# The first load of a batched matmul: 2 KB packets in place of 8 KB ones

## The chip, the cores and the metric

One core of a Trainium2 chip. The time is the device time of one execution in microseconds. A ratio of two kernels is the mean time of one kernel's fast runs over that of the other's of the same rounds, so it isn't quite the ratio of the medians that are quoted beside it.

## The reference

```python
batch, m, k, n = 16, 512, 512, 512
a: (batch, k, m) float32;  b: (batch, k, n) float32
out = np.matmul(a.transpose(0, 2, 1), b).astype(np.float32)
```

It reads 2 x 16.8 MB and writes 16.8 MB.

## The kernel before

SyncE issues all loads and stores. VectorE casts them to bf16, TensorE multiplies, ScalarE copies PSUM to SBUF. The batches go in pairs. The first pair is loaded batch by batch, in four loads of 1 MB (`a` of batch 0, `b` of batch 0, `a` and `b` of batch 1), so that the compute can begin early. In these loads partition p holds the rows 4p to 4p + 3 of k, a contiguous run of 8 KB:

```python
R, RV = 8, 4
in0_v = [x.rearrange("batch (p r) m -> batch p r m", r=RV) for x in (a, b)]
...
for j in range(2):        # j = 0: a, j = 1: b, of batch 0
    nc.sync.dma_start(x_ts[j][:, 0:RV, :], in0_v[j][0]).then_inc(s_f[j], 16)
for j in range(2):        # of batch 1
    nc.sync.dma_start(x_ts[j][:, RV:R, :], in0_v[j][1]).then_inc(s_x[j], 16)
for n in range(2, 2 * pairs):
    if n >= NX:           # from the third pair on: wait until a buffer has been cast
        nc.sync.wait_ge(s_in, n - NX + 1)
    ...                   # 2 MB loads of 16 KB runs
```

All outputs are issued after the last load.

## Time and profile before

| | before |
|---|---|
| time, median of the first 3 runs | 123.19 us (123.08 to 123.24) |
| span of the profiled run | 121.4 us |
| DMA packets, bytes | 4864, 50.33 MB |
| share of the 16 DMA engines | 97.7% |
| busiest compute engine | PE, 51% |

Each digit of the DMA row on the page is the busy share of one of 40 equal slices, in tenths; the row of GB/s below it is what they moved. The DMA row is 9 from end to end here. The reading, which the experiments below bear out for this kernel, is that a microsecond more of transfer is a microsecond more of time (where the last output landed 4.07 us later, the time grew by 3.84), and all else is hidden behind it. The lines themselves are shown in the prediction.

### The profile page before, as it was taken

Reading aid. Unit: us, or ns where it says so; the run is one execution under the profiler, and the core shown is the slowest. Engines: PE = TensorE matmul, PEld = TensorE weight load, DVE = VectorE, ACT = ScalarE, POOL = GpSimd, SP = SyncE. Lnnn points to the kernel's source line nnn. Section 1 sums busy time; section 2 is a strip of 40 time slices with the busy share of each in tenths; the row PEclk is TensorE's granted clock in tenths of the full one; section 3 lists DMA queues with packets and bytes.
Section 4 is the critical chain, followed back from the end, with each engine's and each line's share of the span. In section 5 each row is a group of like instructions: output and inputs, shape, how many; then the busy total and the mean of one; then the engine's idle time right before and its main releaser. Section 6 shows DMA issues by size and latency. Waiting matters only on the chain.

```text
span 121.4 us, 1204 instructions
## 1 busy us (share of the span) xinstructions
PE 61.7 (51%) x480; PEld 35.0 (29%) x480; DVE 38.1 (31%) x48; ACT 32.2 (27%) x41; POOL 0.2 (0%) x4
## 2 busy tenths in 40 slices
PE   0007829099379559959919979989800000000000
PEld 0002314066156225536515636655400000000000
DVE  0061160864284090484265347492000000000000
ACT  4000423302900920390560084190009200000000
POOL 0000000000000000000000000000000000000000
PEclk9999999999999967999995999999995555555555
DMA  2999999999999999999999999999999999999994
GB/s 57 424 432 429 467 432 432 432 432 432 432 432 432 432 432 427 432 432 416 432 427 427 432 432 402 432 427 427 429 429 432 429 429 432 421 424 429 429 424 208
DMA packets 4864, 50.33 MB, mean 415 GB/s; under 512 B 384, under 2 KB 384, under 8 KB 384
## 3 DMA queue, kind: packets, MB, share of 16 engines
q1 hardware_dynamic: 4864, 50.33, 97.7%
HBM read 33.55 MB, written 16.78 MB: 415 GB/s over the span
## 4 chain that ended last, share of the span: by engine, by line
DMA 63%; DVE 6%; issue 3%; ACT 2%; SPq 2%; ACTq 1%
DMA x<-in_b_dram 53%; DMA out_dram<-o 10%; DVE bbf L118 3%; DVE abf L118 3%; ACT o L181 2%; SPq L74 1%; ACTq L70 1%; SPq L72 1%; SPq L80 0%; DVE done L124 0%; ACT done L186 0%; SPq L219 0%; SPq L70 0%
## 5 line engine op out<-in xcount | busy, mean ns | idle before, releaser
L156 PE MATMUL ps<-bbf,abf 64*128 64x512 bf16 x448 | 53.0, 393 | 13.6 <-PEq L151 13.6
L156 PEld LDWEIGHTS ps<-bbf,abf 64*128 64x128 bf16 x448 | 31.3, 112 | 35.3 <-issue 20.6
L181 ACT COPY o<-ps 128x1024 f32<-128x1024 f32 x28 | 26.3, 1026 | 45.9 <-PE ps L156 37.0
L118 DVE CAST abf<-x 128x2048 bf16<-128x2048 f32 x14 | 17.1, 1224 | 17.5 <-PE ps L156 13.5
L118 DVE CAST bbf<-x 128x2048 bf16<-128x2048 f32 x14 | 17.1, 1225 | 14.6 <-DMA x<-in_b_dram 14.6
L136 PE MATMUL ps<-bbf,abf 128*128 128x512 bf16 x32 | 8.7, 433 | 12.4 <-PEq L134 12.4
L136 PEld LDWEIGHTS ps<-bbf,abf 128*128 128x128 bf16 x32 | 3.7, 121 | 16.9 <-issue 14.8
L175 ACT COPY o<-ps 128x1024 f32<-128x1024 f32 x4 | 4.0, 1012 | 15.9 <-PE ps L136 15.9
L99 DVE CAST abf<-x 128x2048 bf16<-128x2048 f32 x2 | 2.5, 1228 | 11.2 <-DMA x<-in_a_dram 5.8
L99 DVE CAST bbf<-x 128x2048 bf16<-128x2048 f32 x2 | 2.5, 1225 | 1.2 <-DMA x<-in_b_dram 1.2
L186 ACT ACTIVATE done<-done 1x1 uint32<-1x1 uint32 x8 | 1.6, 197 | 0.0
L175 ACT ACT_TABLE_LOAD x1 | 1.3, 1283 | 0.9 <-SPq L70 0.9
L124 DVE MEMSET done<- 1x1 f32 x14 | 0.8, 59 | 0.0
L103 DVE MEMSET done<- 1x1 f32 x2 | 0.1, 59 | 0.0
L208 POOL MEMSET const-bfloat16-1.0<- 128x1 bf16 x1 | 0.1, 102 | 0.0
L208 POOL MEMSET const-uint8-127<- 128x1 uint8 x1 | 0.1, 102 | 0.0
L208 POOL MEMSET const-float32-0.0<- 128x1 f32 x1 | 0.1, 99 | 0.2 <-issue 0.2
L208 POOL MEMSET const-float32-1.0<- 128x1 f32 x1 | 0.1, 99 | 0.0
## 6 DMA issues: line engine op xcount, KB each, us to landing
x<-in_a_dram SPq DMA_DIRECT2D x7, 2048.0 KB, 12.2
x<-in_b_dram SPq DMA_DIRECT2D x6, 2048.0 KB, 15.9
out_dram<-o SPq DMA_DIRECT2D x3, 4096.0 KB, 21.7
x<-in_b_dram SPq DMA_DIRECT2D x4, 1024.0 KB, 12.1
out_dram<-o SPq DMA_DIRECT2D x2, 2048.0 KB, 29.3
x<-in_a_dram SPq DMA_DIRECT2D x2, 1024.0 KB, 6.8
```

Of the source, the lines that this page charges most:

```text
L70: with tc.tile_critical(no_gpsimd_drain=True):
L72: nc.sync.dma_start(x_ts[j][:, 0:RV, :], in0_v[j][0]).then_inc(s_f[j], 16)
L74: nc.sync.dma_start(x_ts[j][:, RV:R, :], in0_v[j][1]).then_inc(s_x[j], 16)
L99: nc.vector.tensor_copy(out=bf_ts[0][:], in_=x_ts[j][:, u * RV:(u + 1) * RV, :]).then_inc(s_cast, 1)
L118: nc.vector.tensor_copy(out=(bbf_ts if n % 2 else abf_ts)[v][:], in_=x_ts[n % NX][:, v * RV:(v + 1) * RV, :],).then_inc(s_cast, 1)
L124: nc.vector.memset(dve_done[:, n:n + 1], 0.0).then_inc(s_in, 1)
L136: mm = nc.tensor.matmul(ps_ts[0][h][:, t % 2, :], a_m[:, r, t], bbf_ts[0][:, r, :], start=(r == 0), stop=(r == RV - 1),)
L156: mm = nc.tensor.matmul(ps_ts[g][h][:, t % 2, :], a_m[:, t], bbf_ts[v][rows, r, :], start=(v == 0 and r == 0), stop=(v == V - 1 and r == R ...
L175: nc.scalar.copy(out=o_ts[0][:, g, 2 * h:2 * h + 2, :], in_=ps_ts[0][h][:]).then_inc(s_ev[h], 1)
L181: ev = nc.scalar.copy(out=o_ts[i % NO][:, g, 2 * h:2 * h + 2, :], in_=ps_ts[g][h][:])
L186: nc.scalar.memzero(act_done[:, i:i + 1]).then_inc(s_out, 1)
L208: nc = _bacc.Bacc("TRN2", target_bir_lowering=False, num_devices=1)
```

## The change

The intent is a gentler start: the very first load of the kernel runs on idle DMA engines (0 GB/s up to 1.9 us), and smaller packets could complete sooner there. The cap of 4 * M = 2048 bytes on a contiguous run cuts this one load into a packet per row: 512 packets of 2 KB where there had been 128 of 8 KB. Bytes, addresses and order of the loads stay as they were.

```diff
         for j in range(2):
-            nc.sync.dma_start(x_ts[j][:, 0:RV, :], in0_v[j][0]).then_inc(s_f[j], 16)
+            nc.sync.dma_start(
+                x_ts[j][:, 0:RV, :], in0_v[j][0], max_dma_last_dim=None if j else 4 * M
+            ).then_inc(s_f[j], 16)
```

## The prediction

> **What bounds the kernel now.** I read the busy table first, then the 40 slices, to see whether one resource is full from end to end.
>
> ```profile
> PE 61.7 (51%) x480; PEld 35.0 (29%) x480; DVE 38.1 (31%) x48; ACT 32.2 (27%) x41; POOL 0.2 (0%) x4
> ...
> DMA  2999999999999999999999999999999999999994
> GB/s 57 424 432 429 467 432 432 432 432 432 432 432 432 432 432 427 432 432 416 432 427 427 432 432 402 432 427 427 429 429 432 429 429 432 421 424 429 429 424 208
> DMA packets 4864, 50.33 MB, mean 415 GB/s; under 512 B 384, under 2 KB 384, under 8 KB 384
> ## 3 DMA queue, kind: packets, MB, share of 16 engines
> q1 hardware_dynamic: 4864, 50.33, 97.7%
> ```
>
> No compute engine is busy for much more than half of the span. The 16 DMA engines are busy in every slice but the first and the last, at about 430 GB/s, and 97.7% over the whole span. 50.33 MB at 430 GB/s is 117.0 us of the 121.4 us span. The other 4.4 us are the start before data flows at full rate and the tail after the last packet. So the end is set by two things only: when each DMA engine gets going, and how long its fixed list of packets takes. The chain of waits agrees: 63% of it is transfers, and its earliest stretch is the issue of the first six loads, one after the other.
>
> Then the start, in the timeline and in a table of short windows (columns of the latter: window, length, busy time of PE, PEld, DVE, ACT, POOL, clock, DMA share, GB/s).
>
> ```profile
> 0.94 0.39 SPq L72 DMA_DIRECT2D x<-in_a_dram  x1
> 1.39 0.42 SPq L72 DMA_DIRECT2D x<-in_b_dram  x1
> 1.86 0.42 SPq L74 DMA_DIRECT2D x<-in_a_dram  x1
> 2.33 0.66 SPq L74 DMA_DIRECT2D x<-in_b_dram  x1
> ...
> 5.78 1.23 DVE L99 CAST abf<-x 128x2048 bf16<-128x2048 f32 x1 [5.78 <-DMA x<-in_a_dram]
> 8.19 1.23 DVE L99 CAST bbf<-x 128x2048 bf16<-128x2048 f32 x1 [1.18 <-DMA x<-in_b_dram]
> ...
> 9.71 5.07 PE L136 MATMUL ps<-bbf,abf 128*128 128x512 bf16 x16 [9.71 <-PEq L134]
> ...
> 16.10 0.33 SPq L80 DMA_DIRECT2D x<-in_a_dram  x1
> ```
>
> ```profile
> 1.50:1.90 0.40, 0.00 (x0) 0.00 (x0) 0.00 (x0) 0.40 (x1) 0.00 (x0) 1.00 0.00 0
> 1.90:2.20 0.30, 0.00 (x0) 0.00 (x0) 0.00 (x0) 0.28 (x1) 0.00 (x0) 1.00 1.09 164
> 2.20:2.50 0.30, 0.00 (x0) 0.00 (x0) 0.00 (x0) 0.00 (x0) 0.00 (x0) 1.00 0.65 109
> 2.50:2.80 0.30, 0.00 (x0) 0.00 (x0) 0.00 (x0) 0.00 (x0) 0.00 (x0) 1.00 0.73 218
> 2.80:3.10 0.30, 0.00 (x0) 0.00 (x0) 0.00 (x0) 0.00 (x0) 0.00 (x0) 1.00 0.35 137
> 3.10:3.40 0.30, 0.00 (x0) 0.00 (x0) 0.00 (x0) 0.00 (x0) 0.00 (x0) 1.00 1.03 437
> ```
>
> The first load is issued at 0.94 us. Nothing moves until 1.9, and from 1.9 to 3.1 the engines move only (164 + 109 + 218 + 137) x 0.3 = 188 KB where 430 GB/s would have moved 516 KB. From 3.1 on the rate is full. So the ramp loses 0.76 us. The packet records of the trace show what that ramp is made of: the first packets start between 1.97 and 2.72 us, and several take 0.8 to 1.16 us each, where the 8 KB packet takes 309 ns in steady running.
>
> [...] an 8 KB packet takes 309 ns and a 16 KB packet 611, so 2 x 309 - 611 = 7 ns is the fixed part. [...] the 1 MB loads land in issue order, about 2.4 us apart (5.78, then 8.19). [...] In the trace each of these loads counts 16 completions. So both kernels give every engine the same 64 KB of the first a; only the cut into packets changes. [...]
>
> **The change, part by part.** In the kernel before, partition p holds rows 4p to 4p + 3 of the first a, one run of 8 KB. The change caps a run at 4M = 2048 bytes, one row. It moves the same bytes to the same places: no instruction of any compute engine changes, and no other DMA. The first a becomes 512 packets in place of 128. The page should show 4864 + 384 = 5248 packets.
>
> (a) Fixed cost per packet. With 7 ns fixed and (309 - 7) / 4 = 75.5 ns for the bytes, an estimated 82.5 ns a packet. Each engine now has 32 x 82.5 = 2.64 us instead of 8 x 309 = 2.47: **+0.17 us**. All 16 engines work side by side, so it counts once. It lies on the path, because the engines have no idle time later in which to make it up.
>
> (b) [...] The out transfers of this kernel have 512 packets too. Their issue instructions take 403, 507 and 870 ns for the first three, which are all out of the way 1.87 us after the first began; the loads with 128 packets take 327 to 433 ns late in the kernel. So 1536 descriptors were taken in 1.87 us, 1.2 ns each at most, and 384 more cost at most 0.47 us. [...] I take **+0.2 us**, between 0 and 0.47.
>
> (c) A gentler ramp. Smaller first packets complete sooner, and an engine with a slow first packet might lose less. The most that this can give is the 0.76 us of the ramp. But the slow packets all end close to 3.0 to 3.1 us, whether they began at 1.98 or at 2.65, as though they waited for one common event, and a smaller packet would wait for it too. I take **-0.15 us**.
>
> Sum: 0.17 + 0.2 - 0.15 = +0.22 us, so 123.19 + 0.22 = **123.4 us**.
>
> What lies off the path: when the first a lands. Even if it lands 0.4 us later, its cast (1.23 us from 5.78) ends at about 7.4, before the first b arrives at 8.19, and the first matmul waits for the latter's cast. [...] The cast chain then issues the next load at 16.10, while what was issued in the first 4 us (8.4 MB) keeps the DMA engines fed until 22.8: 6.7 us of slack, far more than any shift here.
>
> **The rivals.** Rival 1: the 2 KB packets start much faster, most of the ramp goes and the transfer time stays: -0.6 us, 122.6. For it speak first packets of up to 1.16 us; against it, their common end. Rival 2: [...] If the spread of 0.75 us in first starts (1.97 to 2.72) grew fourfold, the last engine would start 2.2 us late and never catch up: 125.5. Against it speak the issue times of the out transfers in (b). [...] Rival 4: the change is absorbed, because the early loads run far ahead of the compute: 123.2. The full DMA slices speak against it: with no idle slot between start and end there is nothing to absorb into, though it would look nearly the same in the time.
>
> **Range and chances.** The parts give -0.4 at the good end ((a) paid, (b) nil, two thirds of the ramp saved) and +0.8 at the bad end ((a) doubled, (b) at its limit), so 122.8 to 124.2 with a little room. 2% of 123.19 is 2.46 us. A gain of that size isn't there: the whole ramp is 0.76 us, and the time from the issue to the first packet is not touched. [...] So faster 0.005, same 0.975, slower 0.02.
>
> **What would show it right or wrong.** Right: 5248 packets; the first a landing within half a microsecond of 5.78; the landing of the first b, and every later landing, shifted by nearly the same amount as the end; steady slices unchanged near 430 GB/s; 2 KB packets of some 80 to 85 ns once running. Wrong: (a) falls if these packets take well over 85 ns in steady running; (b) if the first packets of the last engines start over half a microsecond later; (c) if the windows from 1.9 to 3.1 us carry far more than 188 KB. The claim that the shift passes to the end undiminished falls if the first b lands later but the last out lands as before. The prediction as a whole would be wrong if a feed gap opened near 22 us, or if the second load's issue were held up by the first for microseconds.

The sum came to 0.17 + 0.2 - 0.15 = +0.22 us, 123.4 us. (a) is an estimate from the durations of 309 and 611 ns, and the counts per engine (64 KB; 8 or 32 packets) are estimates too, an even split of each load over its 16 completions. For (b), +0.2 is my choice under the 0.47 us that I estimated from the issue times of the stores.

## The result, and the profile after

The changed kernel takes 123.39 us (123.34 to 123.44, 6 runs), the kernel before 123.17 us (123.08 to 123.24, 6 runs) in the same rounds. The ratio is 1.0019, with a 95% interval of 1.0006 to 1.0032: the same within 2%, and slower by about 0.2 us.

First the page of the changed kernel, the lines that answer to those shown of before:

```profile
PE 65.0 (53%) x480; PEld 35.4 (29%) x480; DVE 38.0 (31%) x48; ACT 32.2 (26%) x41; POOL 0.2 (0%) x4
...
DMA  2999999999999999999999999999999999999994
GB/s 69 405 431 428 434 431 431 431 431 431 431 431 431 431 431 431 431 431 431 431 431 431 431 431 431 431 431 420 425 428 428 431 428 428 428 423 423 431 431 175
DMA packets 5248, 50.33 MB, mean 414 GB/s; under 512 B 384, under 2 KB 384, under 8 KB 896
...
q1 hardware_dynamic: 5248, 50.33, 97.5%
```

There are 384 packets more (the class under 8 KB grew from 384 to 896, the 512 packets of 2 KB). The DMA row is the same, full from the second slice on, and the steady rate is the same (433 GB/s from 20 to 60 us against 429). The second slice is lower, 405 in place of 424 GB/s: that is where the first load is under way.

Then the timeline of its start:

```profile
0.94 0.43 SPq L73 DMA_DIRECT2D x<-in_a_dram  x1
1.43 0.49 SPq L73 DMA_DIRECT2D x<-in_b_dram  x1
...
6.11 1.23 DVE L102 CAST abf<-x 128x2048 bf16<-128x2048 f32 x1 [6.11 <-DMA x<-in_a_dram]
8.53 1.23 DVE L102 CAST bbf<-x 128x2048 bf16<-128x2048 f32 x1 [1.19 <-DMA x<-in_b_dram]
...
17.93 0.33 SPq L83 DMA_DIRECT2D x<-in_a_dram  x1
```

The first cast begins when the first a has landed: at 6.11 us, 0.33 later than before. The first b's cast is 0.34 later too (8.53 against 8.19). By the records of completions in the trace, the next four loads are later by 0.33 to 0.36 us, and the last output lands at 120.76 instead of 120.41, 0.35 later. So whatever happened, it happened within the first load; from there the shift of the last landing goes undiminished to the end. The next load is issued at 17.93 instead of 16.10, which looks large and means nothing: what was issued before lasts until about 23 us, and the kernel before, profiled again, issued it at 17.18.

The windows of the start, changed kernel, with the columns as in the prediction:

```profile
1.90:2.20 0.30, 0.00 (x0) 0.00 (x0) 0.00 (x0) 0.28 (x1) 0.00 (x0) 1.00 0.36 89
2.20:2.50 0.30, 0.00 (x0) 0.00 (x0) 0.00 (x0) 0.00 (x0) 0.00 (x0) 1.00 0.45 171
2.50:2.80 0.30, 0.00 (x0) 0.00 (x0) 0.00 (x0) 0.00 (x0) 0.00 (x0) 1.00 0.98 232
2.80:3.10 0.30, 0.00 (x0) 0.00 (x0) 0.00 (x0) 0.00 (x0) 0.00 (x0) 1.00 0.83 259
3.10:3.40 0.30, 0.00 (x0) 0.00 (x0) 0.00 (x0) 0.00 (x0) 0.00 (x0) 1.00 1.01 341
```

From 1.9 to 3.1 us this is (89 + 171 + 232 + 259) x 0.3 = 225 KB (188 GB/s) against 188 KB (157 GB/s) before: a little more, not less. But read it with care: a packet counts as a whole where it starts, so 8 KB packets are booked early. And from 3.1 to 3.4 us the rate is 341 GB/s where it had been 437. One profile can't say what this is made of.

### The profile page after: what moved, and what is told of

Read it like the earlier page. It is cut to its first block, busy times and chain, and to the rows that moved or that the text cites. A ratio compares the mean times of both kernels' runs of the same rounds, so it can differ in the third digit from the quotient of the medians.

```text
span 121.7 us, 1204 instructions
## 1 busy us (share of the span) xinstructions
PE 65.0 (53%) x480; PEld 35.4 (29%) x480; DVE 38.0 (31%) x48; ACT 32.2 (26%) x41; POOL 0.2 (0%) x4
## 2 busy tenths in 40 slices
DMA packets 5248, 50.33 MB, mean 414 GB/s; under 512 B 384, under 2 KB 384, under 8 KB 896
## 3 DMA queue, kind: packets, MB, share of 16 engines
q1 hardware_dynamic: 5248, 50.33, 97.5%
## 4 chain that ended last, share of the span: by engine, by line
DMA 45%; DVE 7%; PE 4%; issue 3%; ACT 2%; ACTq 1%
DMA x<-in_b_dram 35%; DMA out_dram<-o 10%; PE ps L139 4%; DVE abf L121 4%; DVE bbf L121 3%; ACT o L184 2%; ACTq L71 1%; DVE done L127 0%; ACT done L189 0%
## 5 line engine op out<-in xcount | busy, mean ns | idle before, releaser
L139 PE MATMUL ps<-bbf,abf 128*128 128x512 bf16 x32 | 11.9, 552 | 12.8 <-PEq L137 12.8
L139 PEld LDWEIGHTS ps<-bbf,abf 128*128 128x128 bf16 x32 | 4.2, 136 | 20.0 <-issue 19.4
```

Source lines behind the costliest of these rows:

```text
L139: mm = nc.tensor.matmul(ps_ts[0][h][:, t % 2, :], a_m[:, r, t], bbf_ts[0][:, r, :], start=(r == 0), stop=(r == RV - 1),)
```

## The experiments

The trace has, for each load, the time at which each of the 16 DMA engines completed its share. In the first profile of the changed kernel these 16 times for the first a fell into two groups of eight, 5.13 to 5.25 and 5.89 to 6.09 us, where before they lay together, 5.32 to 5.76. The mean was the same (5.59 and 5.58). That suggested the **slowest-engine theory**: the smaller packets spread the starts of the engines, and the last one sets the end. The rival was the **packet-cost theory**: each packet has a fixed cost, on all engines alike. In the expectations below, "start-up theory" is the first one's general form: the cost belongs to the start and not to the packets.

The comparison runs of the kernel before differed between the three sets: 123.12 to 123.84 us in the first, 123.10 to 123.36 in the second, 123.09 to 123.28 in the third. The first set's times can't resolve 0.2 us; its traces can.

### Other packet sizes for the first a: 4 KB and 1 KB

```diff
-                x_ts[j][:, 0:RV, :], in0_v[j][0], max_dma_last_dim=None if j else 4 * M
+                x_ts[j][:, 0:RV, :], in0_v[j][0], max_dma_last_dim=None if j else 8 * M   # e1: 4 KB
+                x_ts[j][:, 0:RV, :], in0_v[j][0], max_dma_last_dim=None if j else 2 * M   # e2: 1 KB
```

> First a in 256 packets of 4 KB. Slowest-engine theory (the late eight engines set the end; they start later and carry the fixed cost per packet): last landing of the first a between the 5.76 us of before and the 6.09 us of the change, about 5.85 to 5.95; time +0.05 to +0.15 us. Packet-cost theory (all of the +0.2 us is a fixed cost per packet, even on all engines): a third of it for 128 more packets instead of 384, +0.07 us, and all 16 completions of the first a shift by the same.

> First a in 1024 packets of 1 KB. Slowest-engine theory: the last engine's first packet starts later again (over 3.0 us instead of 2.86), last landing 6.4 to 6.7 us, time +0.6 to +0.8 us, with the two halves of the engines further apart than the 0.8 us of the change. Packet-cost theory: 896 more packets cost 896/384 of 0.22, +0.5 us, with the halves no further apart than in the change.

4 KB: 123.28 us (before 123.37), ratio 0.9992 (0.9973 to 1.0012). The first a landed at 5.95 us, again in two groups (5.04 to 5.21 and 5.75 to 5.95), as the slowest-engine theory had expected. The time says nothing at this scatter. 1 KB: 123.47 us, ratio 1.0011 (0.9991 to 1.0032), not resolved either. But its trace speaks: the last landing was 6.08 us, far from the 6.4 to 6.7 that the slowest-engine theory asked for (and 0.32 later than before, not the 0.5 of the packet-cost theory), and the engines lay closer together (5.60 to 6.08) than in the changed kernel, with four times as many packets as in the 4 KB run. A spread that grows with the number of packets isn't there.

### Small packets in the second load instead of the first

```diff
-                ... in0_v[j][0], max_dma_last_dim=None if j else 4 * M
+                ... in0_v[j][0], max_dma_last_dim=4 * M if j else None
```

> First a in 8 KB packets as before, first b (the second load) in 2 KB ones. [...] Slowest-engine theory: only the fixed cost per packet is left: starts of 2 KB packets in the changed kernel lie 80 ns apart and of 8 KB ones 305, so 32 x 80 - 8 x 305 = +0.12 us; the first a lands at 5.76 as before and no gap opens between the halves of the engines. Packet-cost theory: the full +0.22 us, since it doesn't matter which load has the small packets. Start-up theory in its strict form (all of the cost is in the start): +0.0 us.

The first b now runs in 2 KB packets on engines that are already streaming (419 GB/s from 3.1 to 5.0 us). Timeline of this run:

```profile
5.85 1.23 DVE L101 CAST abf<-x 128x2048 bf16<-128x2048 f32 x1 [5.85 <-DMA x<-in_a_dram]
8.38 1.23 DVE L101 CAST bbf<-x 128x2048 bf16<-128x2048 f32 x1 [1.30 <-DMA x<-in_b_dram]
```

By the mean over the 16 engines, this b completed 2.55 us after the a ahead of it; in the kernel before it took 2.44. So 24 more packets per engine cost 0.11 us where nothing starts up: close to the 0.12 that the slowest-engine theory left for them, half of the packet-cost theory's 0.22, and not the 0 of the strict start-up theory. No groups formed (5.35 to 5.83 for the a, 7.91 to 8.36 for the b). The time, 123.31 us with a ratio of 0.9995 (0.9975 to 1.0015), is again too scattered to add anything.

### All other loads in 2 KB packets

The first a keeps its 8 KB packets, and every other load gets the cap of 4 * M.

> The other way round and made large: the first a in 8 KB packets, all 31 MB of the other loads in 2 KB ones. Measures the fixed cost per packet by itself. From 80 ns between starts at 2 KB against about 607 at 16 KB (75.9 per 2 KB): 992 packets per engine x 4.1 ns = +4 us if 80 ns holds; with the 7 ns of the packets' durations as the fixed cost, 82.5 - 76.4 = 6.1 ns each, +6 us. If this stays under +1 us, a fixed cost per packet explains nothing of the change's +0.22 us and the whole of it is in the start.

127.20 us, ratio 1.0311 (1.0285 to 1.0337). Its page:

```profile
DMA packets 18432, 50.33 MB, mean 401 GB/s; under 512 B 384, under 2 KB 384, under 8 KB 16256
```

And the rate in the middle of the load stage, first of the kernel before, then of this one:

```profile
20.00:60.00 40.00, 30.30 (x258) 17.79 (x257) 20.17 (x25) 14.04 (x20) 0.00 (x0) 0.96 1.00 429
```

```profile
20.00:60.00 40.00, 29.34 (x237) 16.70 (x237) 19.16 (x25) 13.46 (x18) 0.00 (x0) 0.91 1.05 409
```

The last column falls from 429 to 409 GB/s, with the DMA engines still busy throughout (1.05). So the longer issue instructions of this run (up to 4.95 us) didn't leave them without work. By an even split there are (18432 - 4864) / 16 = 848 more packets on each engine. The last output landed 4.07 us later, as expected for 80 ns a packet; that is 4.8 ns for each packet added; by the ratio the time rose by 3.84 us, 4.5 ns a packet; and the second load of the run before gives 0.11 us / 24 = 4.6 ns. **The fixed cost of a packet, as these two runs measure it, is 4.5 to 4.8 ns.** For the change that makes 24 x 4.6 = 0.11 us. This is the packet-cost theory's mechanism, but half the size that it needs for the whole of 0.22.

### The first load alone, 8 KB and 2 KB

What is the rest? In all traces so far, some packets in flight in the first microsecond are stretched, up to 1.16 us for an 8 KB packet that otherwise takes 309 ns, and whatever their size, most of those over 0.4 us end between 2.7 and 3.3 us. (The first expectation below says that all end between 3.0 and 3.3. That is too strong: in the run with small packets in the second load, four of 8 KB ended at 2.56 to 2.76.) To see whether the loads issued right behind hold the first one up, they were kept back until it had landed:

```diff
         for j in range(2):
+            if j:
+                nc.sync.wait_ge(s_f[0], 16)
             nc.sync.dma_start(x_ts[j][:, 0:RV, :], in0_v[j][0]) ...
```

> The first a in 8 KB packets, and the second load issued only when all of the first a has landed. In five kernels so far the stretched early packets all end between 3.0 and 3.3 us, whatever their size. Interference theory (the descriptors of the loads issued behind it hold the first one up): alone, no packet ends stretched near 3.1 us; early engines land at about 1.97 + 2.44 + 0.2 = 4.6 us and late ones at about 5.3 us. Warm-up theory (a common event some 1.1 us after the first packet, such as a first access): the stretched packets still end near 3.1 us and the first a lands near 5.76 us, as before. The time itself gets about 2 us worse in both, by the gap.

> The same with the first a in 2 KB packets. Interference theory: no stretched packets near 3.1 us; early engines land at about 2.04 + 2.56 + 0.2 = 4.8 us, late ones at about 2.86 + 2.56 + 0.2 = 5.6 us. Warm-up theory: the landings are those of the changed kernel, 5.13 to 6.09 us. If the late eight engines start at 2.6 or later here too, the late start is not the work of the loads behind.

The times were 125.43 and 125.71 us (one run each), worse by the gap as expected. The interference theory fell: alone, eight 8 KB packets are still stretched to over 1.0 us and end between 3.04 and 3.18 us, and the first a lands at 5.47 to 5.69 us. But the warm-up theory, in the form of a single event at the kernel's start, doesn't fit either. Windows of the 8 KB run around its second load, issued at 5.70 us onto engines that had gone idle:

```profile
5.70:6.60 0.90, 0.00 (x0) 0.00 (x0) 0.89 (x1) 0.00 (x0) 0.00 (x0) 1.00 0.00 0
6.60:7.80 1.20, 0.00 (x0) 0.00 (x0) 0.33 (x1) 0.00 (x0) 0.00 (x0) 1.00 0.93 164
7.80:9.80 2.00, 0.00 (x0) 0.00 (x0) 0.00 (x0) 0.00 (x0) 0.00 (x0) 1.00 1.01 426
```

Nothing for 0.9 us, then busy engines (0.93) that start only 164 GB/s worth of packets for 1.2 us, then the full rate. That is the start of the kernel over again: the window of 1.2 us moved 157 GB/s in the kernel before. So the ramp was there at both starts on idle engines of this run, and not only at the first; its cause is open. (It isn't tied to idle engines alone: two runs below have stretched packets right behind running ones, in one of them of up to 0.80 us.) With 2 KB packets the first a alone landed at 5.61 to 5.84 us, without the two groups.

### A small transfer ahead of the first load

```diff
-            nc.sync.dma_start(x_ts[j][:, 0:RV, :], in0_v[j][0]).then_inc(s_f[j], 16)
+            if j == 0:
+                for p0, p1 in ((0, 16), (16, P)):
+                    nc.sync.dma_start(
+                        x_ts[0][p0:p1, 0:RV, :], in0_v[0][0, p0:p1]
+                    ).then_inc(s_f[0], 16)
+            else:
+                nc.sync.dma_start(x_ts[1][:, 0:RV, :], in0_v[1][0]).then_inc(s_f[1], 16)
```

with the three waits on this semaphore raised by 16.

> The first a, in 8 KB packets, in two transfers: partitions 0 to 15 (one packet per engine), then 16 to 127. If the late start of eight engines comes from the number of descriptors that must be made before theirs, all sixteen first packets start within 0.2 us of 1.97 and the first a lands 0.2 to 0.4 us earlier, time -0.2 to -0.4 us. If it is fixed per transfer or belongs to the engines, eight engines still start near 2.6 us, and the time is +0.0 to +0.2 us for one issue more.

124.24 us, ratio 1.0082 (1.0067 to 1.0098): worse by 1.0 us, neither of the two expectations. The first half of the idea worked: all 16 engines started between 1.97 and 2.15 us, and these 16 packets took 352 to 371 ns, not stretched. Then the second transfer went slowly. Windows of this run:

```profile
1.90:3.10 1.20, 0.00 (x0) 0.00 (x0) 0.00 (x0) 0.28 (x1) 0.00 (x0) 1.00 1.08 225
3.10:7.00 3.90, 0.00 (x0) 0.00 (x0) 0.00 (x0) 0.00 (x0) 0.00 (x0) 1.00 0.96 298
7.00:9.00 2.00, 0.00 (x0) 0.00 (x0) 1.23 (x1) 0.00 (x0) 0.00 (x0) 1.00 0.99 418
```

Most of its first packets were stretched until 3.3 to 3.6 us, and most of its packets after that took 340 to 540 ns instead of 309, until it was through near 7 us (298 GB/s from 3.1 to 7.0). So this transfer of partitions 16 to 127 wasn't as fast as one of all 128. Whether that comes from their number, from the partition at which it begins or from the transfer just ahead of it, no run has separated; this split isn't a way to a faster start.

### Both kernels again, and the packets made more and smaller

> The changed kernel once more, for the scatter of a second profile. Slowest-engine theory: the landings of the first a fall again into two groups of eight, near 5.2 and 6.0 us, and the last completion of the kernel is later than that of before by as much as the last landing of the first a. If the groups are an accident of one run, they are gone; time +0.1 to +0.3 us either way.

> The kernel before against itself, for the scatter: time ratio 1.000. The last landing of the first a near 5.76 us; the four profiles with 8 KB packets gave 5.69 to 5.83.

> The changed kernel, third profile. Packet-cost theory, with what the other runs have shown (a 1 MB load in mid-stream takes 2.44 us in 8 KB packets and 2.55 in 2 KB ones): the last landing of the first a near 5.76 + 0.11 = 5.87 us, the completions not in two groups; time +0.1 us. Slowest-engine theory: two groups again, last near 6.1 us, time +0.2 us or more.

The changed kernel again: 123.30 us beside 123.25 for before, ratio 1.0002 (0.9989 to 1.0016), and 123.41 beside 123.17, ratio 1.0021 (1.0008 to 1.0035). The kernel before against itself: 123.22 beside 123.17, ratio 1.0003 (0.9989 to 1.0016). The first casts in the timelines, of the changed kernel's second and third profile, and of the second profile of the kernel before:

```profile
5.91 1.23 DVE L102 CAST abf<-x 128x2048 bf16<-128x2048 f32 x1 [5.91 <-DMA x<-in_a_dram]
```

```profile
6.06 1.23 DVE L102 CAST abf<-x 128x2048 bf16<-128x2048 f32 x1 [6.06 <-DMA x<-in_a_dram]
```

```profile
5.75 1.23 DVE L99 CAST abf<-x 128x2048 bf16<-128x2048 f32 x1 [5.75 <-DMA x<-in_a_dram]
```

The two groups of eight were gone in both repeats of the changed kernel (completions 5.43 to 5.89 and 5.52 to 6.04 us). So the first half of the slowest-engine theory, that the smaller packets spread the starts, fell as I had read it from one profile: the groups come in some executions, and the repeats landed late without them.

Its second half, that the last engine sets the end, held, and one number shows it. In the first profile of the changed kernel the 16 completions of the last output were still in two groups (119.97 to 120.28 and 120.58 to 120.76). Their mean was only 0.12 us later than before, about the packets' fixed cost of 0.11; the last of them was 0.35 later. How far the engines lie apart differs between executions (for the first a of the changed kernel 0.96, 0.46 and 0.52 us), and in this pair the time went with the last one (123.44 us against 123.09 in the profiled runs).

```diff
+ max_dma_last_dim=None if j else M      # e8: first a in 512-byte packets
+ max_dma_last_dim=4 * M                 # e9: all four 1 MB loads of the first pair in 2 KB packets
```

> The first a alone, in 2048 packets of 512 bytes, 128 per engine. Packet-cost theory: a fixed 3.4 ns for each of 120 more packets than before, +0.41 us on the first a, last landing near 6.2 us, and +0.4 us in time. Descriptor-generation theory (the 1.2 ns each that the prediction gave as its limit, for 1920 more): up to +2.3 us. Start-up theory (all of the change's cost is scatter or start): +0.1 us.

> The change's own packets four times over: the first four loads of 1 MB (both halves of the first a and b) in 2 KB packets. Packet-cost theory: 4 x 0.11 = +0.4 us in time, each of the four landings later than before by 0.11 us more than the one ahead of it. Start-up theory: +0.1 us, as in the changed kernel.

My expectation for the 512-byte run divided 0.11 us by 32 packets; it is 24 that are added, so the 4.6 ns from above ask for 120 x 4.6 = 0.55 us. Measured: 123.85 us, ratio 1.0047 (1.0033 to 1.0061), +0.58 us. The first a landed at 6.31, 0.55 us later than before. The descriptor-generation theory at its limit, 1.2 ns for each of 1920 packets (+2.3), is excluded. Not all of this run is clean. Its timeline:

```profile
1.43 1.91 SPq L72 DMA_DIRECT2D x<-in_b_dram  x1
...
6.33 1.23 DVE L101 CAST abf<-x 128x2048 bf16<-128x2048 f32 x1 [6.33 <-DMA x<-in_a_dram]
```

The second load's issue took 1.91 us instead of 0.42, and some of its first packets were stretched as well (up to 0.80 us). The five times spread from 123.60 to 124.27, and in the profiled one, the slowest, the last output landed 1.15 us later, not 0.55. So the first landing fits the packet cost; that the time does too is partly chance.

Four loads in 2 KB packets: 123.68 us, ratio 1.0043 (1.0029 to 1.0057), +0.53 us. Timeline:

```profile
6.01 1.23 DVE L101 CAST abf<-x 128x2048 bf16<-128x2048 f32 x1 [6.01 <-DMA x<-in_a_dram]
8.55 1.23 DVE L101 CAST bbf<-x 128x2048 bf16<-128x2048 f32 x1 [1.32 <-DMA x<-in_b_dram]
```

Here one run shows both parts. The first a landed at 5.99 us, +0.23 against the first profile of before. Each of the three loads behind it took 0.11 us more than in the kernel before (by the mean of the 16 completions 2.55, 2.56 and 2.59 us where it had been 2.44, 2.44 and 2.48). 0.23 + 3 x 0.11 = 0.56; the fourth load did land 0.57 us later (13.70 against 13.13).

**What the change costs, put together.** Five profiles have the first a in 8 KB packets as in the kernel before (before, again, second load small, all others small, alone): last landing 5.69 to 5.83 us, mean 5.76. Five have it in 2 KB packets (the change three times, four loads, alone): 5.84 to 6.09, mean 5.97. The two sets touch but don't overlap; the difference of the means is 0.21 us. 0.11 of it is the fixed cost of 24 packets. The other 0.10 us lies in the start, and five profiles of each, which scatter by 0.14 to 0.25 us within their set, hardly resolve it. By the mean of the 16 completions in place of the last the sets lie at 5.597 and 5.732 us, 0.135 apart, which leaves 0.03. The rest of the 0.10 is how far the engines lay apart in these executions.

One thing is regular there: the first packet of all starts at 1.96 to 1.97 us in the five with 8 KB packets and at 2.04 to 2.05 in the five with 2 KB, 0.08 us later, and the issue takes 434 ns instead of 392. (From the beginning of the issue to the first packet it is 1.03 us in the trace of the kernel before and 1.09 in the first one of the changed kernel, from the end of the issue 0.63 and 0.66; the prediction took this time as untouched.) It is nearly the same step for any number of packets: with the first a in 4 KB, 1 KB and 512-byte packets the first one started 0.05, 0.08 and 0.09 us later than with 8 KB, behind an issue of 433 ns in all three. Whether this step is what arrives at the end, through a ramp whose stretched packets end at about the same time in both, no run has shown.

No run was faster than the kernel before by more than the scatter.

## Why the prediction was right

**The bound and the path: right.** The DMA engines are full to the end, and nothing was absorbed: the shift at the first landing (0.33 us in the first pair of profiles) and at the last output (0.35) are nearly the same, and in the runs made to enlarge it the time grew as the transfers did (+0.53 and +3.84 us). The rival of the absorbed change is excluded by these. The late landing of the first a costs the compute nothing that counts: the next load is issued at 16.10 and 17.18 us in two profiles of the kernel before, at 17.34 to 17.93 in three of the changed one, all well ahead of the 22.8 us up to which the DMA engines have work. The signs that the prediction named held too: 5248 packets, the same steady rate, no gap near 22 us, and a second issue that took 0.49 us in place of 0.42.

**(a), the fixed cost per packet: right in kind, too large.** It was put at 7 ns and +0.17 us; it is 4.6 ns and +0.11 us. The 7 ns came from durations (309 and 611 ns). Durations are longer than the pace, as if neighbouring packets of one engine overlapped by some nanoseconds: the 2 KB packets last 84 ns, about as predicted, but 32 of them need 2.55 us, 80 ns each, and eight of 309 ns need 2.44. The pace should have been read from the landings of successive loads. What the 4.6 ns are made of was not shown.

**(b), more packets to issue: small, and not as it was taken.** +0.2 was taken, for a cost that grows with the number of packets. What is seen is the first packet, 0.08 us later in each of five profiles, and that step hardly grows: it is 0.05 to 0.09 us for 128 to 1920 more packets. What grows is the issue of the second load: 0.42, 0.46, 0.49, 0.57 and 1.91 us behind a first load in packets of 8, 4, 2, 1 and 0.5 KB. The bound of 1.2 ns a packet also left out the fourth store's issue, which took 5.50 us in the same trace.

**(c), the gentler ramp: no gain was seen.** It was to give 0.15 us back. In the first profile the window totals looked like that (188 GB/s against 157), but the two repeats moved less in the same 1.2 us (118 and 99 GB/s against 157), some of it by the booking of whole packets. The landings, which have no such bias, show a net loss in the start, 0.10 us by the last engine and 0.03 by the mean, where (b) and (c) together said 0.05. No run separates the two terms. The doubt that was noted there held in the main: most of the packets stretched to over 0.4 us end between 2.7 and 3.3 us whatever their size (in the kernel before, between 3.04 and 3.26, a little later than the 3.0 to 3.1 that the prediction read).

So the path and the order of size were right, and that the sum, +0.22, met the +0.22 of the first comparison to the hundredth is luck: (a) was 0.06 too large, (b) and (c) were not measured one by one, and the three comparisons of the two kernels give ratios of 1.0019, 1.0002 and 1.0021, that is +0.02 to +0.26 us, on average +0.17. A slip in the range changes nothing: its good end comes to +0.17 - 0.51 = -0.34, not -0.4.

**The other rivals.** The much faster start (122.6) didn't come. The fourfold spread of starts (125.5) is excluded by the last landing, at most 6.09 us in three profiles.

## What to carry to other kernels

When the DMA engines are full from end to end, as in this kernel, count the packets that a change adds on one engine and multiply by their fixed cost; here it was 4.6 ns a packet, 0.11 us for 1 MB in 2 KB instead of 8 KB, beside 0.03 to 0.10 us at the start that stayed unexplained. Take the pace of packets from the landings of successive loads, not from packet durations, which came out longer here (84 ns against 80). Look at all 16 completions of a load, their mean as well as the last: here the mean showed the work (+0.12 us), and the last set the time (+0.35). And don't build a mechanism on one profile of a start-up: repeat it first, and enlarge the suspected cost until it stands clear of the scatter.
